# Sums of a seven-product FFN moved from VectorE into the accumulation of TensorE

## The chip, the cores and the metric

The kernel runs on one core of a Trainium2 chip. The metric is the device time of one execution in microseconds (us), lower is better; a comparison goes by the median of several runs. A separate execution is profiled, and all views of the profile and of its trace come from that one. PE is TensorE (PEld its weight loads), DVE is VectorE, ACT is ScalarE, POOL is GpSimd, SP is the engine that issues most DMAs.

## The reference

One decoder layer in float32 over x of 512 tokens x 1024: a half-step SwiGLU FFN, a token mixer of two kinds of recurrent heads, and a second half-step FFN, each with a norm before and after. The change is in the FFNs and in the step from the mixer to the second FFN.

```python
D_MODEL = 1024; SEQ = 512; D_FF = 2816
def rms_norm(x, g):
    xf = x.astype(jnp.float32)
    y = xf * lax.rsqrt(jnp.mean(xf * xf, axis=-1, keepdims=True) + EPS)
    return (y * g.astype(jnp.float32)).astype(x.dtype)

def swiglu_ffn(x, w_in, w_out):
    gate, up = jnp.split(x @ w_in, 2, axis=-1)
    return (jax.nn.silu(gate) * up) @ w_out

# per layer l
x = x + 0.5 * rms_norm(swiglu_ffn(rms_norm(x, norm_pre[l, 0]), ffn1_w_in[l], ffn1_w_out[l]), norm_post[l, 0])
mixed = token_mixer(rms_norm(x, norm_pre[l, 1]), w_mix_in[l], ...)
x = x + rms_norm(mixed, norm_post[l, 1])
x = x + 0.5 * rms_norm(swiglu_ffn(rms_norm(x, norm_pre[l, 2]), ffn2_w_in[l], ffn2_w_out[l]), norm_post[l, 2])
```

## The kernel before

**Products in two parts.** A float32 operand is split into a high part, rounded to the type that TensorE multiplies quickly (fp32r), and a low part, the rest. A product is three passes: high by high, high by low, low by high. For weights, ACT casts the high part (line 245) and DVE subtracts to get the low one (line 247); `split` does this, and four places (`WBUF`) in one tile hold split weights in turn. The raw weights come by DMA into rings of buffers.

**Seven products per pair.** The 2816 columns of gate and of up are taken in 11 pairs of 128-column chunks (t = 0 to 10). For one pair, the input is cut in two halves of tokens (256 each) and two halves of the model dimension (512 each), and the weights in a (upper rows, gate), b (upper rows, up), c (lower rows, gate), d (lower rows, up). The 2 x 2 block product is made of seven products p1 to p7 instead of eight, in Winograd's form, with sums of input blocks (s1 to s4, made once by `sums`) and sums of weights. The weight sums are made in place in the raw buffers (line 261): for t below `HEAD` = 3 by GpSimd, later by DVE. Pair 0 is made in the ordinary way (products c1 to c4 and e1 to e4), while the sums of the input are still in the making. One product is 24 matmuls of 128 x 128 by 256 (line 562) in `prod`; its result is one PSUM bank (128 x 512: two chunks of columns by 256 tokens). p2 adds to p1's bank and p4 to p5's.

**What follows a product** is in `after`. `h0` and `h1` are the two token halves of hf, the hidden activations of the pair. Before the change, in the names of the code (P1 for the result of p1):

- after p1, ACT copies P1 to h1; after p2, ACT puts Silu(P1 + P2) to h0;
- after p5, DVE writes u = P5 - P1 to SBUF;
- after p6, DVE writes q = P6 + u to SBUF, and h1 = q - P7;
- with p6 and p3 there, DVE adds q to p3's bank; with p2 there too, h0 = that bank times h0 is put on a list (`later`) that `lag` empties at the next product;
- after p4, DVE subtracts h1 from p5's bank, ACT takes its Silu in place, and h1 is multiplied by it, again by way of `later`.

**What sets the order.** The products come in the hand-written list `ORDER`; `HEADS` is its beginning. p4 of a pair stands in the next pair. In the steady pairs (t from 4 on) the order is p1, p4 of t - 1, p3, p5, p7, p6, p2. A scheduler puts each engine's instructions in an order before the run, with the program's order as the priority; each engine runs its own queue strictly in order, and semaphores make it wait for the others. PSUM has eight banks, handed out as they come free. `weights` works out from the list when each raw buffer's DMA may be issued.

**Between mixer and second FFN** stands `mix_out1`: the second 512 columns of the mixer's output product, for each of four tiles of 128 tokens. `last` runs the matmuls of a tile, then `post1` (the norm after, and x updated in two halves of 512 columns by line 457: first the half in SBUF, `y`, and then the half that still lies in a PSUM bank), then `pre` (the norm before the FFN: two squares summed on ACT, a power on GpSimd, a scaling on DVE). Then `ffn_head` begins the second FFN with c1, c3 and so on. For the last tile c1 runs meanwhile, and c3 follows the transposes of the third tile.

Of the kernel before, what the change touches and what calls it, by code (L numbers as in the profile page):

```python
# [38 lines left out]


HEAD = 3
HEADS = [("c1", 0), ("c3", 0), ("c2", 0), ("c4", 0), ("p1", 1), ("e1", 0), ("e3", 0)]
HEADS += [("e2", 0), ("p1", 2), ("p2", 1), ("e4", 0), ("p2", 2)]
ORDER = HEADS + [(p, 1) for p in ("p7", "p5", "p3", "p6")] + [("p5", 2), ("p7", 2), ("p3", 2), ("p4", 1), ("p6", 2)]
for _t in range(HEAD, PAIRS):
    if _t == HEAD:
        ORDER += [("p1", _t), ("p3", _t), ("p5", _t), ("p4", _t - 1)] + [(p, _t) for p in ("p7", "p6", "p2")]
    else:
        ORDER += [("p1", _t), ("p4", _t - 1)] + [(p, _t) for p in ("p3", "p5", "p7", "p6", "p2")]

# [35 lines left out]
class Layer:  # L88
# [257 lines left out]
    def sums(self, i, src):  # L346


        nc = self.nc
        v = slice((i % 2) * P, (i % 2 + 1) * P)  # L350
        f = [x[:, :, v] for x in self.xf]
        sub = lambda out, a, b: nc.vector.tensor_tensor(out, a, b, op=ALU.subtract)
        hi = lambda dst, src: nc.scalar.copy(dst[0][:, :, v], src)
        lo = lambda dst, src: sub(dst[1][:, :, v], src, dst[0][:, :, v].bitcast(F32))
        p1, p0 = self.turn(src, 1), self.turn(src, 0)
        a22 = self.hf[:, 10 + i, :].rearrange("p (c t) -> p c t", c=KH)
        s1, s2, s3, s4 = self.left["e1"], self.sq[2], self.sq[1], self.sq[0]
        a21, two = self.left["e1"], self.left["e2"]
        hi(a21, p0)
        hi(two, p1)  # L360
        nc.scalar.copy(a22, p1)
        lo(a21, p0)
        self.lowed = lo(two, p1)
        yield
        sub(p1, p0, a22)
        sub(p0, f[0], p0)
        hi(s3, p0)
        lo(s3, p0)
        yield
        sub(p0, f[0], p1)  # L370
        hi(s1, p1)
        lo(s1, p1)
        yield
        hi(s2, p0)
        sub(p1, f[1], p0)
        lo(s2, p0)
        yield
        hi(s4, p1)
        lo(s4, p1)
        yield  # L380
# [30 lines left out]
        self.pow = nc.gpsimd.tensor_tensor(r, b, self.nhalf[:, :1], op=ALU.pow)  # L411
        yield r

    def pre(self, i, g):

        r, xn = self.root(i)
        for h in range(2):
            self.scaled(i, g, r, xn, h)
        return xn

    def root(self, i):

        x = self.xs[:, i, :]
        *_, r = self.rms([x[:, :512], x[:, 512:]])
        if i % 2:
            xn = self.hf[:, 16:18, :].rearrange("p a t -> p (a t)")
        else:
            xn = self.sp.tile([P, D], F32, tag="xn", bufs=1, name=self.nm("xn"))
        return r, xn
# [16 lines left out]
    def post1(self, i, y, parts, rms, pieces, g, out=None):  # L446

        nc = self.nc
        for ps, v in pieces:
            parts.append(ps)  # L450
            next(rms)
            o = ps if out is None else out[:, v]
            nc.vector.tensor_tensor(o, ps, g[:, 512 + v.start : 512 + v.stop], op=ALU.mult)
        r = next(rms)
        for h, v in enumerate((y, pieces[0][0] if out is None else out)):
            x = self.xs[:, i, 512 * h : 512 * h + 512]
            added = nc.vector.scalar_tensor_tensor(x, v, r, x, op0=ALU.mult, op1=ALU.add)
        self.added = [self.square, added]
# [9 lines left out]
    def last(self, mm, ys, pieces, g, after, trans, head, out=lambda i: ()):  # L468


        for i in range(NT):
            for left in mm(i):
                if i == NT - 1 and left == 2:
                    trans(i - 2)
            self.post1(i, *ys[i], pieces(i), g, *out(i))
            after(i)
            if i == 2:
                trans(0)
        head(trans)

# [51 lines left out]
    def open_ffn(self, ctx):  # L534

        hp = self.hpool = ctx.enter_context(self.tc.tile_pool(name=self.nm("hp"), bufs=1))
        self.hf = hp.tile([P, NF, T], F32, name=self.nm("hf"))
        self.xf = [self.hf[:, j : j + 2, :].rearrange("p a (b t) -> p (a b) t", t=HALF) for j in (NF - 4, NF - 2)]
        sq = [hp.tile([P, 2 * D + PAD], F32R, tag="s", bufs=3, name=self.nm("sq")) for _ in range(3)]
        self.sq = [self.both(self.place(t, LATE)) for t in sq]  # L540
        xq = [self.both(x) for x in self.xh]
        self.stay = [self.place(t, NEXT) for t in sq]
        self.left = {"p1": xq[0], "p2": xq[1], "p4": xq[3], "p5": xq[2], "p6": self.sq[2], "p7": self.sq[1], "p3": self.sq[0]}
        self.left.update({"c1": xq[0], "c2": xq[1], "c3": xq[0], "c4": xq[1]})
        self.left.update({"e1": xq[2], "e2": xq[3], "e3": xq[2], "e4": xq[3]})
        self.gs, self.held, self.copies = [], {}, []
        self.hs, self.bank, self.later, self.u, self.q, self.had = deque(), {}, deque(), {}, {}, set()

    def prod(self, p, t, feed=True):

        w, left = self.held.pop("c" + p[1]) if p[0] == "e" else self.pull(feed), self.left[p]
        if p[0] == "c":
            self.held[p] = w
        into = {"p2": "p1", "p4": "p5", "c2": "c1", "c4": "c3", "e2": "e1", "e4": "e3"}.get(p, p)
        ps = self.bank[into, t] = self.bank.get((into, t)) or self.ps()
        first = into == p
        wb = self.both(w)
        for n, (b, d) in enumerate(((0, 0), (1, 0), (0, 1)) if p == "c1" else ((0, 0), (0, 1), (1, 0))):
            for a in range(2):
                c, v = slice(HALF * a, HALF * (a + 1)), slice(P * a, P * (a + 1))  # L560
                for k in range(KH):
                    self.nc.tensor.matmul(  # L562
                        ps[:, c], wb[b][:, k, v], left[d][:, k, :],
                        start=first and a + n + k == 0, stop=n == 2 and k == KH - 1, skip_group_check=True,
                    )
        if p[0] == "p" or p == "e2":
            self.drop(w)
        self.had.add((p, t))
# [8 lines left out]
    def after(self, p, t):  # L577
# [5 lines left out]
        if p in ("c2", "e2"):  # L583
            nc.scalar.activation(h0 if p == "c2" else h1, self.two_by(bank[p[0] + "1", t]), AF.Silu)
        elif p in ("c4", "e4"):
            h = h0 if p == "c4" else h1
            self.later.append(lambda: tt(h, self.two_by(bank[p[0] + "3", t]), h, ALU.mult))
        elif p == "p1":
            nc.scalar.copy(h1, self.two_by(bank["p1", t]))  # L589
        elif p == "p2":  # L590
            nc.scalar.activation(h0, self.two_by(bank["p1", t]), AF.Silu)
        elif p == "p4":
            ps = bank["p5", t]
            tt(self.two_by(ps), self.two_by(ps), h1, ALU.subtract)
            nc.scalar.activation(ps, ps, AF.Silu)
            self.later.append(lambda: tt(h1, self.two_by(ps), h1, ALU.mult))
        elif p == "p5":
            u = self.u[t] = self.st("u")
            tt(self.two_by(u), self.two_by(bank["p5", t]), h1, ALU.subtract)
        elif p == "p6":  # L600
            u = self.u.pop(t)
            q = self.q[t] = self.st("q")
            tt(q, bank["p6", t], u, ALU.add)
            tt(h1, self.two_by(q), self.two_by(bank["p7", t]), ALU.subtract)
        if p in ("p6", "p3") and {("p6", t), ("p3", t)} <= had:
            tt(bank["p3", t], self.q.pop(t), bank["p3", t], ALU.add)
        if p in ("p6", "p3", "p2") and {("p6", t), ("p3", t), ("p2", t)} <= had:
            self.later.append(lambda: tt(h0, self.two_by(bank["p3", t]), h0, ALU.mult))

    def lag(self):  # L610
        while self.later:
# [115 lines left out]
    def ffn_in(self):  # L727

        for p, t in ORDER[len(HEADS) :]:
            self.feed()  # L730
            self.lag()
            self.prod(p, t)
            self.after(p, t)
            if t == PAIRS - 1 and p in ("p7", "p6"):
                self.hs.append(self.h_tile(len(self.hs)))
        self.feed()
        self.lag()
# [277 lines left out]
    def ffn_items(self, name, w_in, w_out):  # L1015
# [5 lines left out]
        for t in range(1, PAIRS):  # L1021
            if t >= HEAD:
                v1, v3 = ("p1", t), ("p4", t - 1)
            elif t > 1:
                v1, v3 = ("p3", t - 1), ("p6", t - 1)
            else:
                v1, v3 = ("p1", 1), ("p1", 2)
            for at, o, i in ((("p5", t), "a", "d"), (("p6", t), "a", "c"), (v1, "a", "b"), (v3, "b", "d")):
# [9 lines left out]
        own = {("p1", t): [load(t, r) for r in "abdc"] for t in range(2, PAIRS)}  # L1038
        own["c1", 0] = [load(t, r, None if (t, r) == (0, "d") else name) for t in range(2) for r in "acbd"]

        stay = {"c1": 1, "c3": 2, "c4": 0}
        for p, t in ORDER:
            if p[0] == "e":
                continue
# [596 lines left out]
def layer(tc, aps):  # L1641
    with ExitStack() as ctx:
# [10 lines left out]
        def norm(i, row=None):  # L1653
            if i == 0 and row is not None:
                gp[0] = L.gain("gpre", pre[row : row + 1, :])
            xn[i] = L.pre(i, gp[0])

        def root(i):

# [76 lines left out]
```

## Time and profile before

| what | value |
|---|---|
| median of 3 runs | 943.95 us (943.27 to 944.35) |
| the profiled execution's own time | 944.65 us |
| its span, first to last instruction | 942.9 us |
| granted TensorE clock in it | 0.999 of full speed |
| PE, PEld busy | 934.1 us (99%), 900.4 us (95%) |
| DVE, ACT, POOL busy | 779.7 us (83%), 490.8 us (52%), 120.9 us (13%) |
| share of the chain that ended last | PE 62%, no other engine over 1% |
| HBM read, written | 92.85 MB, 2.10 MB |

How to read it: the slices divide the span in 40 equal parts, a digit being the busy tenths of an engine. A row of the timeline has the start (us from the span's start), the length, the engine, the line of the kernel, the operation, the tile written and those read, the shape and a count; in brackets the idle time of that engine ahead of it and who ended it. The row of a group of matmuls is longer than their pitch by the last one's way through the array, so ends are read from the next row's start. In the list of waits each row has the total, the number and the longest. The first FFN's input products run from about 12 to 226 us, the second's from about 608 to 820 us.

### The profile page before, as it was taken

How to read it: one execution, taken by the hardware profiler on the slowest of the kernel's cores; microseconds unless marked ns; L12 is line 12 of the kernel's file. 1: busy time of each engine (PE TensorE's matmuls, PEld its weight loads, DVE VectorE, ACT ScalarE, POOL GpSimd, SP SyncE). 2: the span in 40 equal slices, each digit the busy share in tenths (PEclk: the TensorE clock that was granted, in tenths of full speed). 3: DMA queues.
4: the chain of work that ended last, by engine and by line, in shares of the span. 5: the costliest groups of instructions: out<-in, count | busy, mean ns of one | idle time of the engine just before them, and what ended most of it. 6: DMA issues, size and time to landing. Idle time of an engine off the chain costs nothing.

```text
span 942.9 us, 18101 instructions
## 1 busy us (share of the span) xinstructions
PE 934.1 (99%) x7507; PEld 900.4 (95%) x7507; DVE 779.7 (83%) x1056; ACT 490.8 (52%) x695; POOL 120.9 (13%) x176
## 2 busy tenths in 40 slices
PE   9999999999999999999999999999999999999997
PEld 7999999999999999998887888899999999999997
DVE  6799989999888876698846665689998999998884
ACT  7645444456456467956632444664444444655541
POOL 2530000000001046200011310363100000000101
PEclk9999999999999999999999999999999999999999
DMA  9244333323352024321212124324333333223212
GB/s 318 86 135 134 110 116 113 112 90 90 99 171 90 24 85 126 107 67 47 88 46 67 46 90 140 103 71 132 115 113 106 119 113 112 68 90 128 75 46 90
DMA packets 81677, 96.13 MB, mean 102 GB/s; under 512 B 4117, under 2 KB 61497, under 8 KB 81594
## 3 DMA queue, kind: packets, MB, share of 16 engines
q1 hardware_dynamic: 81306, 94.44, 31.7%
q8 instruction: 59, 0.97, 0.4%
q10 hardware_dynamic: 288, 0.52, 0.2%
q14 instruction: 24, 0.20, 0.1%
HBM read 92.85 MB, written 2.10 MB: 101 GB/s over the span
## 4 chain that ended last, share of the span: by engine, by line
PE 62%; ACT 1%; DVE 1%; POOL 0%; issue 0%; POOLq 0%; DVEq 0%; ACTq 0%
PE ps L562 22%; PE ps L835 8%; PE ps L496 6%; PE ps L151 5%; PE ps L843 5%; PE ps L153 4%; PE ps L152 4%; PE ps L1226 2%; PE ps L506 1%; PE ps L319 1%; PE ps L1400 0%; PE ps L1311 0%; PE ps L1480 0%; PE ps L1507 0%; PE ps L1266 0%; ACT junk L406 0%
## 5 line engine op out<-in xcount | busy, mean ns | idle before, releaser
L245 ACT CAST w<-raw 128x1024 fp32r<-128x1024 f32 (+1 forms) x232 | 239.1, 1035 | 252.9 <-PE ps L562 102.5
L247 DVE TENSOR_TENSOR w<-raw,w 128x1024 fp32r<-128x1024 f32 (+1 forms) x232 | 286.1, 1240 | 35.8 <-ACT w L245 35.5
L562 PE MATMUL ps<-xq,w 128*128 128x256 f32 x2016 | 238.5, 277 | 0.0
L562 PEld LDWEIGHTS ps<-xq,w 128*128 128x128 f32 x2016 | 233.8, 188 | 0.2 <-ACT hf L589 0.2
L562 PE MATMUL ps<-sq,w 128*128 128x256 f32 x1440 | 170.5, 277 | 0.0
L562 PEld LDWEIGHTS ps<-sq,w 128*128 128x128 f32 x1440 | 166.8, 188 | 0.0
L835 PE MATMUL ps<-w,hs 128*128 128x256 f32 x1056 | 124.2, 276 | 0.0
L835 PEld LDWEIGHTS ps<-w,hs 128*128 128x128 f32 x1056 | 121.7, 188 | 0.0
L261 DVE TENSOR_TENSOR raw<-raw,raw 128x1024 f32<-128x1024 f32 x64 | 82.3, 1285 | 0.6
L151 PE MATMUL ps<-w,xq 128*128 128x512 f32 x192 | 78.9, 411 | 0.1
L152 PE MATMUL ps<-w,xq 128*128 128x512 f32 x192 | 74.8, 390 | 0.0
L153 PE MATMUL ps<-w,xq 128*128 128x512 f32 x192 | 74.8, 391 | 0.0
L407 POOL TENSOR_SCALAR col<-col 128x1 f32<-128x1 f32 x24 | 9.0, 374 | 493.7 <-ACT junk L406 493.6
L496 PE MATMUL ps<-xq,w 128*128 128x256 f32 x480 | 56.4, 278 | 0.0
L496 PEld LDWEIGHTS ps<-xq,w 128*128 128x128 f32 x480 | 55.2, 188 | 0.5 <-issue 0.5
L843 PE MATMUL ps<-w,hs 128*128 128x256 f32 x432 | 51.9, 276 | 0.0
L261 POOL TENSOR_TENSOR raw<-raw,raw 128x1024 f32<-128x1024 f32 x16 | 44.2, 2763 | 50.7 <-DVE w L247 41.4
L843 PEld LDWEIGHTS ps<-w,hs 128*128 128x128 f32 x432 | 50.3, 188 | 0.0
L754 ACT CAST hs<-hf 128x1024 fp32r<-128x1024 f32 x34 | 35.7, 1050 | 25.7 <-PE ps L843 14.1
L151 PEld LDWEIGHTS ps<-w,xq 128*128 128x128 f32 x192 | 36.1, 188 | 8.2 <-issue 0.9
L153 PEld LDWEIGHTS ps<-w,xq 128*128 128x128 f32 x192 | 36.0, 188 | 8.2 <-DVE xq L326 0.3
L755 DVE TENSOR_TENSOR hs<-hf,hs 128x1024 fp32r<-128x1024 f32 x34 | 41.6, 1224 | 1.5 <-ACT hs L754 1.5
(255 smaller groups left out, 1167.1 us busy)
## 6 DMA issues: line engine op xcount, KB each, us to landing
raw<-in_ffn_w_in_dram SPq DMA_DIRECT2D x88, 512.0 KB, 3.6
raw<-in_ffn_w_out_dram SPq DMA_DIRECT2D x44, 512.0 KB, 4.1
raw<-in_w_mix_in_dram SPq DMA_DIRECT2D x28, 512.0 KB, 3.6
raw<-in_w_mix_out_dram SPq DMA_DIRECT2D x8, 512.0 KB, 3.6
out_dram<-xs SPq DMA_DIRECT2D x8, 256.0 KB, 2.0
xs<-in_x_dram SPq DMA_DIRECT2D x6, 256.0 KB, 7.0
gpost<-in_norm_post_dram SPq DMA_DIRECT2D x3, 512.0 KB, 4.6
gpre<-in_norm_pre_dram SPq DMA_DIRECT2D x2, 512.0 KB, 4.0
```

Of the source, the lines that this page charges most:

```text
L151: mm(ps, sh, mh, start=start, stop=False, **kw)
L152: mm(ps, sh, ml, start=False, stop=False, **kw)
L153: mm(ps, sl, mh, start=False, stop=stop, **kw)
L245: nc.scalar.copy(hi, raw)
L247: self.low = nc.vector.tensor_tensor(lo, raw, hi.bitcast(F32), op=ALU.subtract)
L261: (nc.vector if late else nc.gpsimd).tensor_tensor(o, o, c, op=ALU.add)
L496: mm(ps[:, u0:u1], w[:, a, k, :], self.xop(k, b, u0, u1), start=k + n + m == 0, stop=k == ND - 1 and n == 2, skip_group_check=True,)
L562: self.nc.tensor.matmul(ps[:, c], wb[b][:, k, v], left[d][:, k, :], start=first and a + n + k == 0, stop=n == 2 and k == KH - 1, skip_grou ...
L754: self.nc.scalar.copy(hi, src)
L755: self.nc.vector.tensor_tensor(lo, src, hi.bitcast(F32), op=ALU.subtract)
L835: mm(out, a[kk][:, i * P : (i + 1) * P], w[:, b, kk, QUARTER * v : QUARTER * (v + 1)], start=begin and c == kk == n == 0, stop=kk == 1 and ...
L843: mm(ps[:, QUARTER * c : QUARTER * (c + 1)], A[a][:, c], B[b], start=begin and c == n == 0, stop=n == 2, skip_group_check=True,)
```

## The change

Five edits go together.

1. From the fifth pair on (t >= `FILLED` = 4), DVE writes P5 - P1 into a PSUM bank, and p6's matmuls start without clearing and add to it. ACT copies the bank to another one, on which p7 is added; p3 is added on the first one. ACT copies the bank of p7 to h1. The left operand of p7 has its sign turned, so that p7 is added where it was subtracted. For t below 4, DVE keeps the sums, in another arrangement with as many operations.
2. The order of products: after the heads p5(1), p5(2), p6(1), p6(2), p3(1), p7(1), p3(2), p4(1), p7(2), and from t = 3 on p1, p5, p4 of t - 1, p6, p2, p3, p7.
3. The tiles of the sums and of the weights kept for pair 0 are renamed, so that they come free in the order in which the output product takes them; the first two tiles for it are made after p3 and p7 of the last pair.
4. Two weight sums of pair 2 are tied to other products: a + b to p2(2) instead of p3(1), b + d to p6(1) as before.
5. In `mix_out1`, the update of x takes the half in the bank first, and the squares of the norm that follows take that half first as well (`turned`).

The diff, without hunks that only move comments:

```diff
 HEAD = 3
+FILLED = 4
 ...
-ORDER = HEADS + [(p, 1) for p in ("p7", "p5", "p3", "p6")] + [("p5", 2), ("p7", 2), ("p3", 2), ("p4", 1), ("p6", 2)]
+ORDER = HEADS + [("p5", 1), ("p5", 2), ("p6", 1), ("p6", 2), ("p3", 1), ("p7", 1), ("p3", 2), ("p4", 1), ("p7", 2)]
 for _t in range(HEAD, PAIRS):
-    if _t == HEAD:
-        ORDER += [("p1", _t), ("p3", _t), ("p5", _t), ("p4", _t - 1)] + [(p, _t) for p in ("p7", "p6", "p2")]
-    else:
-        ORDER += [("p1", _t), ("p4", _t - 1)] + [(p, _t) for p in ("p3", "p5", "p7", "p6", "p2")]
+    ORDER += [("p1", _t), ("p5", _t), ("p4", _t - 1)] + [(p, _t) for p in ("p6", "p2", "p3", "p7")]
 ...
-        s1, s2, s3, s4 = self.left["e1"], self.sq[2], self.sq[1], self.sq[0]
+        s1, s2, s3, s4 = self.left["e1"], self.sq[0], self.sq[2], self.sq[1]
 ...
-        sub(p0, f[0], p0)
+        sub(p0, p0, f[0])
 ...
-    def root(self, i):
+    def root(self, i, turned=False):
         x = self.xs[:, i, :]
-        *_, r = self.rms([x[:, :512], x[:, 512:]])
+        parts = [x[:, :512], x[:, 512:]]
+        *_, r = self.rms(parts[::-1] if turned else parts)
 ...
-        for h, v in enumerate((y, pieces[0][0] if out is None else out)):
+        for h, v in ((1, pieces[0][0]), (0, y)) if out is None else ((0, y), (1, out)):
 ...
-        self.left = {..., "p6": self.sq[2], "p7": self.sq[1], "p3": self.sq[0]}
+        self.left = {..., "p6": self.sq[0], "p7": self.sq[2], "p3": self.sq[1]}
 ...
         into = {"p2": "p1", "p4": "p5", "c2": "c1", "c4": "c3", "e2": "e1", "e4": "e3"}.get(p, p)
+        if p == "p3" and t >= FILLED:
+            into = "p6"
         ps = self.bank[into, t] = self.bank.get((into, t)) or self.ps()
-        first = into == p
+        first = into == p and (t < FILLED or p not in ("p6", "p7"))
 ...
-        elif p == "p5":
+        elif p == "p5" and t < FILLED:
             u = self.u[t] = self.st("u")
             tt(self.two_by(u), self.two_by(bank["p5", t]), h1, ALU.subtract)
+        elif p == "p5":
+            q = bank["p6", t] = self.ps()
+            tt(self.two_by(q), self.two_by(bank["p5", t]), h1, ALU.subtract)
+        elif p == "p6" and t < FILLED:
+            u = self.u[t]
+            tt(u, bank["p6", t], u, ALU.add)
         elif p == "p6":
-            u = self.u.pop(t)
-            q = self.q[t] = self.st("q")
-            tt(q, bank["p6", t], u, ALU.add)
-            tt(h1, self.two_by(q), self.two_by(bank["p7", t]), ALU.subtract)
-        if p in ("p6", "p3") and {("p6", t), ("p3", t)} <= had:
-            tt(bank["p3", t], self.q.pop(t), bank["p3", t], ALU.add)
-        if p in ("p6", "p3", "p2") and {("p6", t), ("p3", t), ("p2", t)} <= had:
-            self.later.append(lambda: tt(h0, self.two_by(bank["p3", t]), h0, ALU.mult))
+            c22 = bank["p7", t] = self.ps()
+            nc.scalar.copy(c22, bank["p6", t])
+        elif p == "p7" and t < FILLED:
+            tt(h1, self.two_by(bank["p7", t]), self.two_by(self.u[t]), ALU.add)
+        elif p == "p7":
+            nc.scalar.copy(h1, self.two_by(bank["p7", t]))
+        elif p == "p3" and t < FILLED:
+            c12 = bank["p6", t] = bank["p3", t]
+            tt(c12, self.u[t], c12, ALU.add)
+        if p in ("p3", "p2") and {("p3", t), ("p2", t)} <= had:
+            self.later.append(lambda: tt(h0, self.two_by(bank["p6", t]), h0, ALU.mult))
 ...
-            if t == PAIRS - 1 and p in ("p7", "p6"):
+            if t == PAIRS - 1 and p in ("p3", "p7"):
                 self.hs.append(self.h_tile(len(self.hs)))
 ...
             elif t > 1:
-                v1, v3 = ("p3", t - 1), ("p6", t - 1)
+                v1, v3 = ("p2", 2), ("p6", 1)
 ...
-        stay = {"c1": 1, "c3": 2, "c4": 0}
+        stay = {"c1": 2, "c3": 0, "c4": 1}
 ...
-            xn[i] = L.pre(i, gp[0])
+            xn[i] = L.pre(i, gp[0], row == 2)
```

More of the change, by code (lines that the diff above doesn't have):

```diff
@@ L412, in rms, with pre @@
         yield r
-    def pre(self, i, g):
-        r, xn = self.root(i)
+    def pre(self, i, g, turned=False):
+        r, xn = self.root(i, turned)
         for h in range(2):
@@ L542, in open_ffn @@
         self.stay = [self.place(t, NEXT) for t in sq]
-        self.left = {"p1": xq[0], "p2": xq[1], "p4": xq[3], "p5": xq[2], "p6": self.sq[2], "p7": self.sq[1], "p3": self.sq[0]}
+        self.left = {"p1": xq[0], "p2": xq[1], "p4": xq[3], "p5": xq[2], "p6": self.sq[0], "p7": self.sq[2], "p3": self.sq[1]}
         self.left.update({"c1": xq[0], "c2": xq[1], "c3": xq[0], "c4": xq[1]})
@@ L546, in open_ffn @@
         self.gs, self.held, self.copies = [], {}, []
-        self.hs, self.bank, self.later, self.u, self.q, self.had = deque(), {}, deque(), {}, {}, set()
+        self.hs, self.bank, self.later, self.u, self.had = deque(), {}, deque(), {}, set()
     def prod(self, p, t, feed=True):
```

## The prediction

> **What bounds the kernel now.** I read the page first: engines, slices, then the chain that ended last.
>
> ```profile
> span 942.9 us, 18101 instructions
> PE 934.1 (99%) x7507; PEld 900.4 (95%) x7507; DVE 779.7 (83%) x1056; ACT 490.8 (52%) x695; POOL 120.9 (13%) x176
> DVE  6799989999888876698846665689998999998884
> ```
>
> PE is busy for all but 8.8 us of the span, and DVE, which the change relieves, is near full in the slices of both FFNs. A busy DVE costs nothing unless PE waits for it, so the next view is the chain in order of time, where the second FFN is one long piece of PE.
>
> ```profile
> 617.59 0.87 PE ps L319 x8
> 618.47 201.99 PE ps L562 x1776
> ...
> 936.74 0.02 issue
> ```
>
> 1776 matmuls in 201.99 us are 0.1137 us each, so one product of 24 takes 2.73 us, with no hole between products. From 936.74 to the end 6.2 us are left, the tail behind the last matmul. So of the 8.8 us without a matmul most lie in the tail and in the start, which the change doesn't touch. PE's waits name what else there is.
>
> ```profile
> PE ps L147 <- POOL ident masks.py:199: 1.5, 1, 1.5
> PE ps L562 <- ACT junk L406: 0.4, 1, 0.4
> PE ps L562 <- ACT xq L339: 0.2, 1, 0.2
> ```
>
> The first, 1.5 us, is the making of the identity at the start. The second, 0.4 us, is at a place that the change edits (below). The whole stock from which it could win is thus about half a microsecond, and whatever new wait it puts on PE is paid in full. 0.2% of the median (943.95) is 1.9 us, about what a measurement of this kernel can tell from no change.
>
> **What the pairs lose on DVE.** Per pair from the fifth (t >= 4) line 581 made seven operations on DVE: the subtraction and the product of p4, u of p5, q and h1 of p6, the sum of p3, the product for h0. Now p6 and p3 accumulate in a bank that holds the sum already, and p7 (its left operand has its sign turned) in a copy, so u's operation goes into a bank, q, h1 and p3's sum go away, and ACT makes two copies more.
>
> ```profile
> 148.45 0.68 DVE L581 TENSOR_TENSOR hf<-q,ps 128x512 f32<-128x512 f32 x1
> 149.05 0.69 DVE L581 TENSOR_TENSOR ps<-q,ps 128x512 f32<-128x512 f32 x1
> 152.28 0.58 ACT L589 COPY hf<-ps 128x512 f32<-128x512 f32 x1
> 155.66 0.58 ACT L595 ACTIVATE ps<-ps 128x512 f32<-128x512 f32 x1 [0.54 <-DVE ps L581]
> ```
>
> One such operation holds DVE for 0.60 us (149.05 less 148.45). Three of them, seven pairs, two FFNs: 25 us off DVE. ACT gets 2 x 14 x 0.58 = 16 us more, where it has 452 us idle. PE's matmuls are as many as before; no row shows a matmul that is dearer when it adds onto a filled bank (each product's later passes add already), so I take nothing. On PE's path the sum of all this is nothing either: DVE's 25 us hide behind PE today.
>
> A copy from bank to bank is not in the trace of before. Its nearest rows are the copy from a bank to hf and the Silu from bank to bank, 0.58 both; I take 0.58. [...]
>
> **The new waits in the steady pairs.** The order becomes p1, p5, p4 of the pair before, p6, p2, p3, p7. Three waits are new.
>
> ```profile
> 141.07 5.60 PE L562 MATMUL ps<-sq,w 128*128 128x256 f32 x48
> 141.27 0.69 DVE L581 TENSOR_TENSOR u<-ps,hf 128x512 f32<-128x512 f32 x1 [0.75 <-PE ps L562]
> 146.51 8.38 PE L562 MATMUL ps<-xq,w 128*128 128x256 f32 x72
> ```
>
> p6 waits for DVE's filling. In this pair p5 ended where p7 began, at 141.07, and DVE was done with u at 141.96: 0.9 us. One product (p4) of 2.73 us lies between, so 1.8 us are to spare. p3 waits for ACT's copy out of the bank it will add to, with p2 between; p7 waits for the same copy, with p2 and p3 between. ACT's row at 152.28 is the copy after p1, which ended at about 152.0 (two products after 146.51): 0.3 + 0.58 = 0.9 us, again under 2.73. Behind DVE's and ACT's waiting instruction stand the next weight halves:
>
> ```profile
> 140.41 1.05 ACT L245 CAST w<-raw 128x1024 fp32r<-128x1024 f32 x1 [1.66 <-PE ps L562]
> 141.88 1.21 DVE L247 TENSOR_TENSOR w<-raw,w 128x1024 fp32r<-128x1024 f32 x1
> 143.12 1.22 DVE L261 TENSOR_TENSOR raw<-raw,raw 128x1024 f32<-128x1024 f32 x1
> ```
>
> Four weight places go round; the cast waits only for PE to leave one, and by the order of the products the half made at 141.88 to 143.09 is that of p1(7), which starts at 149.23: 6.1 us ahead. p5 now follows p1 directly, and its weights are p1's raw plus another, so its cast waits for p1's low half and the sum: 1.05 + 1.22 + 1.22 = 3.5 us after p1's cast instead of 2.73. It is some 0.8 us later, out of 6. Nothing reaches PE. Of the banks a pair takes four, where it took five, so no wait for a bank is added.
>
> **The fifth pair of the first FFN** is where DVE is behind.
>
> ```profile
> 92.10 0.69 DVE L581 TENSOR_TENSOR q<-ps,u 128x512 f32<-128x512 f32 x1
> 96.76 1.23 DVE L261 TENSOR_TENSOR raw<-raw,raw 128x1024 f32<-128x1024 f32 x1
> 97.44 2.88 PE L562 MATMUL ps<-sq,w 128*128 128x256 f32 x24
> 99.37 0.70 DVE L581 TENSOR_TENSOR ps<-ps,hf 128x512 f32<-128x512 f32 x1
> 100.16 2.88 PE L562 MATMUL ps<-xq,w 128*128 128x256 f32 x24
> 116.73 0.70 DVE L581 TENSOR_TENSOR ps<-ps,hf 128x512 f32<-128x512 f32 x1 [0.48 <-PE ps L562]
> ```
>
> p4(3) ended at 97.44 and its subtraction came at 99.37, 1.9 us late. In the new order that slot ends p5(4), and p6(4) begins at 100.16. With the same lag the filling ends at 100.07: just in time. Every sum of raws that the new order pulls ahead of it costs 1.22 us; with one (a += c for p6) PE would stand for 1.2 us. Below nothing it can't go. The lag row itself is the nearest, so I take 0.2 us and keep 0 to 1.3. A pair later the lag is gone (DVE idle before 116.73), and 1.8 us per pair are saved besides.
>
> **The join before the second FFN.**
>
> ```profile
> 607.56 3.00 PE L562 MATMUL ps<-xq,sq 128*128 128x256 f32 x24
> 610.24 0.74 DVE L457 SCALAR_TENSOR_TENSOR xs<-y,col,xs 128x512 f32<-128x512 f32 x1
> 610.39 1.03 PE L319 MATMUL ps<-ident,xn 128*128 128x128 f32 x8
> 610.90 0.75 DVE L457 SCALAR_TENSOR_TENSOR xs<-ps,col,xs 128x512 f32<-128x512 f32 x1
> 611.56 1.22 DVE L247 TENSOR_TENSOR sq<-raw,sq 128x1024 fp32r<-128x1024 f32 x1
> 611.79 3.08 PE L562 MATMUL ps<-xq,sq 128*128 128x256 f32 x24 [0.36 <-ACT junk L406]
> 614.99 1.42 DVE L433 SCALAR_TENSOR_TENSOR hf<-xs,col,gpre 128x512 f32<-128x512 f32 x2 [1.08 <-POOL col L411]
> 617.43 1.03 PE L319 MATMUL ps<-ident,hf 128*128 128x128 f32 x8
> ```
>
> The wait is put down to ACT, but the product c3 begins 0.14 us after DVE's second addition (610.90 + 0.75 = 611.65), the one that reads a bank: the bank is what c3 needs. With the bank's half first it is free at 610.99, before the eight transposes are through (611.26; eight take 0.87 us in the chain above). So c3 starts about 0.5 us sooner. What is late next: c3's low weights end at 612.78, wanted for its last eight matmuls at 613.1; the transposes at 617.43 would come at 616.9 and read what DVE ends at 616.41. Both hold, narrowly. The square that follows reads the half made first (turned), so its time stays. Gain: 0.5 us; from 0 (c3's bank is another) to 0.55. The tail keeps its old order.
>
> **The third pair and before.** The products after the heads are reordered, with as many operations for t < 4 as before. GpSimd's eight sums of raws per FFN come in another order, and those of p5(2) and p6(2) earlier.
>
> ```profile
> 53.01 5.84 POOL L261 TENSOR_TENSOR raw<-raw,raw 128x1024 f32<-128x1024 f32 x2 [8.93 <-DVE col L1074]
> 54.13 2.40 DVE L1078 TENSOR_TENSOR col<-col,col 128x4 f32<-128x4 f32 x1
> 59.59 2.35 DVE L247 TENSOR_TENSOR w<-raw,w 128x1024 fp32r<-128x1024 f32 x2
> 61.48 5.82 PE L562 MATMUL ps<-sq,w 128*128 128x256 f32 x48
> 67.28 3.31 POOL L261 TENSOR_TENSOR raw<-raw,raw 128x1024 f32<-128x1024 f32 x1 [8.42 <-DVE w L247]
> 68.37 4.57 DVE L261 TENSOR_TENSOR raw<-raw,raw 128x1024 f32<-128x1024 f32 x2
> 619.92 0.70 DVE L352 TENSOR_TENSOR ps<-ps,hf 128x512 f32<-128x512 f32 x1
> ```
>
> While GpSimd adds, a DVE operation on 4 columns takes 2.40 us. By the order of splits the first low half of 59.59 is for the product at 61.48: it ends at 60.8, with 0.7 us to spare, and 2.5 us counting that low halves are read in a product's last third. In the new order another of these sums (the one at 67.28) moves to before that product, and two more of line 581's operations (u's of p5(2), and p6(1)'s): 2.4 + 2 x 0.6 = 3.6 us against 2.5. But it leaves 68.37, where a DVE sum took about twice its 1.22. Bounds -0.2 (the third wait in PE's list, should it lie here) to +3.5 (the 3.6 with nothing to spare); I take nothing, as PE stood for nothing that the page lists under the same eight sums before. [...]
>
> **The sum**, against the profiled execution's 944.65 us (span 942.9 and 1.75 around it): -0.5 + 0.2 + 0 = -0.3. The median of the runs is 0.7 lower than that execution, so 943.95 - 0.3 = 943.6 us.
>
> **The rivals.**
> (a) GpSimd's sums and DVE's weights collide about 48 to 65 us, and PE waits there. For: the 0.7 us above, and DVE late by microseconds up to 100 us. Against: the second FFN, whose DVE is less late, and the low half's third. Price 1 to 3.5, less 0.3: 944.7 to 947.2; about 945.5. Chance 0.18, of which 0.12 beyond +1.9.
> (b) Slower in every pair: DVE's queue puts the filling behind a low half and a sum that are released at the same time. It decides from 1.8 us of delay. Price: 0.2 + 1.22 + 1.22 + 0.69 + 0.1 = 3.4 us against 2.73, 0.7 us in each of 14 pairs, 9.8 us: 953. For: the order of DVE's queue is fixed when the program is built, and low halves come every 2.73 us. Against: u, in the same place, began 0.2 us after p5 in the steady pairs. Chance 0.13.
> (c) c3's bank is another, or its weights hold it up: 944.1 us. Chance 0.03; against it, the 0.14 us.
> (d) Faster by over 1.9 us: PE would have to gain what no wait shows, some other hole between matmuls. 0.03, at 941.5.
>
> **How the numbers follow.** The forecast has 0.63; with (c) and the smaller part of (a), 0.72 lie within 0.2%. Slower is (b) and the larger part of (a), 0.25; faster 0.03. The range goes down to the full gain of join and heads with the median's own spread (942.8) and up to the middle of (a) with that spread (946.0); (b), the end of (a) and (d) are left out, about 0.2.
>
> **What would show it.** c3 begins near 611.3 if all before it stays; PE's waits show line 562 behind DVE's filling or ACT's copies for tenths at most; DVE's busy time falls by some 25 us with the span unmoved; ACT's rises by 16. Wrong would be: holes before p6 in each pair (b), holes near 50 to 65 us (a), or c3 still waiting for DVE (c).

## The result

| | median | runs | ratio to before |
|---|---|---|---|
| before | 943.95 us | 943.27 to 945.64, 7 runs | |
| after | 946.78 us | 945.98 to 947.72, 7 runs | 1.0028 (1.0018 to 1.0037) |
| after, run again beside before on another chip | 946.26 us (before 943.59) | 945.94 to 947.13, 6 runs | 1.0029 (1.0018 to 1.0041) |

The change makes the kernel slower, by 2.8 us (0.3%) in the first comparison and by 2.7 in the second. The forecast was 943.6, range 942.8 to 946.0. The profiled execution of after took 946.30 us, with a span of 944.6.

The page of after, engines and slices:

```profile
span 944.6 us, 18076 instructions
PE 933.8 (99%) x7507; PEld 899.4 (95%) x7507; DVE 756.6 (80%) x1014; ACT 504.3 (53%) x723; POOL 118.6 (13%) x176
```

DVE has 42 operations and 23 us less, ACT 28 and 13.5 us more, PE the same matmuls: the change does what it says. None of it was on PE's path. PE's waits show what is:

```profile
PE ps L145 <- POOL ident masks.py:199: 1.5, 1, 1.5
PE ps L565 <- DVE xq L339: 0.6, 1, 0.6
PE ps L565 <- ACT xq L337: 0.5, 2, 0.3
PE ps L565 <- DVE xs L457: 0.5, 1, 0.5
PE ps L565 <- DVE ps L584: 0.4, 1, 0.4
```

The columns are the total, the number and the longest. The last row is the fifth pair's p6, which waits for DVE's filling (line 584 is before's 581). The three above it lie at the join before the second FFN, but for 0.2 of the 0.5 us for ACT's `xq`: that wait ends at 12.0 us, at the head of the first FFN, where the kernel before has it too. (Lines 565, 457, 404, 432, 339, 337 and 245 of after are 562, 457, 406, 433, 341, 339 and 247 of before.)

**Where the 2.6 us lie.** Both kernels were profiled a second time (e9 and e10 below), 943.76 and 946.34 us. Four rows of the same place in each give the account. They are a product of pair 0 at the head of the first FFN, eight transposes after the first FFN, the long piece of the second FFN in the chain, and the last update of x. First before, then after:

```profile
41.74 2.88 PE L562 MATMUL ps<-xq,sq 128*128 128x256 f32 x24
335.65 1.03 PE L319 MATMUL ps<-ident,xn 128*128 128x128 f32 x8
617.61 201.98 PE ps L562 x1776
938.29 0.74 DVE L457 SCALAR_TENSOR_TENSOR xs<-hf,col,xs 128x512 f32<-128x512 f32 x1
span 942.1 us, 18101 instructions
```

```profile
41.69 2.88 PE L565 MATMUL ps<-xq,sq 128*128 128x256 f32 x24
336.21 1.03 PE L317 MATMUL ps<-ident,xn 128*128 128x128 f32 x8
619.63 201.98 PE ps L565 x1776
940.31 0.75 DVE L457 SCALAR_TENSOR_TENSOR xs<-hf,col,xs 128x512 f32<-128x512 f32 x1
span 944.6 us, 18076 instructions
```

| place | after less before |
|---|---|
| start (41.69 - 41.74) | -0.05 |
| first FFN (336.21 - 335.65, less the above) | +0.61 |
| mixer and join (619.63 - 617.61 = 2.02, less 0.56) | +1.46 |
| second FFN (201.98 both) and output (940.31 - 938.29 = 2.02) | 0.00 |
| tail behind the last update (944.6 - 942.1 = 2.5, less 2.02) | +0.5 |
| sum | +2.5 (own times: 946.34 - 943.76 = 2.58) |

The n-th matmul of one trace set against the n-th of the other narrows this down: all of the 0.61 arises between 97 and 115 us, 1.49 us between 604 and 613 us (the mixer ahead of it gives back 0.03), and the steady pairs of both FFNs differ by nothing.

**The join.** The third tile's update, its first square and its scaling, and c1 and c3, before (e9):

```profile
602.05 0.75 DVE L457 SCALAR_TENSOR_TENSOR xs<-y,col,xs 128x512 f32<-128x512 f32 x1 [0.19 <-POOL col L411]
602.71 0.75 DVE L457 SCALAR_TENSOR_TENSOR xs<-ps,col,xs 128x512 f32<-128x512 f32 x1
602.89 0.63 ACT L406 ACTIVATE junk<-xs 128x512 f32<-128x512 f32 x1 [1.47 <-DVE xs L457]
606.27 1.42 DVE L433 SCALAR_TENSOR_TENSOR xn<-xs,col,gpre 128x512 f32<-128x512 f32 x2 [1.62 <-POOL col L411]
606.72 3.00 PE L562 MATMUL ps<-xq,sq 128*128 128x256 f32 x24
610.96 1.77 PE L562 MATMUL ps<-xq,sq 128*128 128x256 f32 x13 [0.36 <-ACT junk L406]
```

and after (e10):

```profile
603.39 0.74 DVE L457 SCALAR_TENSOR_TENSOR xs<-y,col,xs 128x512 f32<-128x512 f32 x1
604.05 0.74 DVE L457 SCALAR_TENSOR_TENSOR xs<-ps,col,xs 128x512 f32<-128x512 f32 x1
604.90 0.63 ACT L404 ACTIVATE junk<-xs 128x512 f32<-128x512 f32 x1 [1.39 <-DVE xs L457]
607.71 2.10 PE L565 MATMUL ps<-xq,sq 128*128 128x256 f32 x16 [0.29 <-ACT xq L337]
608.28 1.42 DVE L432 SCALAR_TENSOR_TENSOR xn<-xs,col,gpre 128x512 f32<-128x512 f32 x2 [2.30 <-POOL col L409]
610.36 1.22 PE L565 MATMUL ps<-xq,sq 128*128 128x256 f32 x8 [0.55 <-DVE xq L339]
612.97 3.06 PE L565 MATMUL ps<-xq,sq 128*128 128x256 f32 x24 [0.51 <-DVE xs L457]
```

Two things are to be seen. DVE takes `xs<-y` before `xs<-ps`, as before: the code names the bank's half first, but the order in which DVE's instructions were put when the program was built does not follow it. ACT's squares do follow the code. The first now reads the half that DVE makes second: it starts 1.51 us after the first update (604.90 - 603.39), where it started after 0.84 (602.89 - 602.05). Square, power, scaling and the next tile's update hang on each other, so each tile adds 0.67 us of its own, and some 0.4 us of it reach the next tile's update: the third tile's update comes 1.34 us later than before (603.39 - 602.05) and its scaling 2.01 us later (608.28 - 606.27). Of both, 0.53 us were there ahead of the join; the 1.48 us that are left of the scaling are the loss.

### The profile page after: what moved, and what is told of

Same layout as the page of the kernel before. It is cut to its first block, busy times and chain, and to the rows that moved or that the text cites. A ratio compares the mean times of both kernels' runs of the same rounds, so it can differ in the third digit from the quotient of the medians.

```text
span 944.6 us, 18076 instructions
## 1 busy us (share of the span) xinstructions
PE 933.8 (99%) x7507; PEld 899.4 (95%) x7507; DVE 756.6 (80%) x1014; ACT 504.3 (53%) x723; POOL 118.6 (13%) x176
## 4 chain that ended last, share of the span: by engine, by line
PE 60%; DVE 2%; ACT 1%; POOL 1%; issue 1%; DVEq 0%; POOLq 0%; ACTq 0%
PE ps L565 22%; PE ps L847 7%; PE ps L497 6%; PE ps L855 5%; PE ps L149 4%; PE ps L151 4%; PE ps L150 4%; PE ps L1238 2%; PE ps L507 1%; ACT junk L404 1%; DVE xs L457 1%; PE ps L317 1%; PE ps L1412 0%; PE ps L1323 0%; PE ps L1519 0%
## 5 line engine op out<-in xcount | busy, mean ns | idle before, releaser
L259 DVE TENSOR_TENSOR raw<-raw,raw 128x1024 f32<-128x1024 f32 x64 | 78.3, 1224 | 1.8
L766 ACT CAST hs<-hf 128x1024 fp32r<-128x1024 f32 x34 | 35.7, 1051 | 20.9 <-PE ps L855 13.5
L259 POOL TENSOR_TENSOR raw<-raw,raw 128x1024 f32<-128x1024 f32 x16 | 42.1, 2637 | 28.3 <-DVE w L245 26.9
```

What stands on the lines that cost most here:

```text
L259: (nc.vector if late else nc.gpsimd).tensor_tensor(o, o, c, op=ALU.add)
L766: self.nc.scalar.copy(hi, src)
```

## The experiments

Each ran with a profile; medians are of 9 to 12 runs (e9 one, e10 six) beside 22 to 32 runs of the kernel before on the same chip (943.88, 943.72 and 943.59 us in the three sets). The expectations speak of the theories by letters: T and F say that the join, the fifth pair and the tail lose by the mechanisms above and below.

### e1: edit 5 undone

```diff
-        for h, v in ((1, pieces[0][0]), (0, y)) if out is None else ((0, y), (1, out)):
+        for h, v in enumerate((y, pieces[0][0] if out is None else out)):
-            xn[i] = L.pre(i, gp[0], row == 2)
+            xn[i] = L.pre(i, gp[0])
```

> The changed kernel with edit 5 undone (update of x and squares in the old order; DVE's instructions come in the same order as with the edit, so this takes away only the turned squares). Theory T: the join loses 1.47 us because the turned squares wait for DVE's second update (0.84 us after the start of that update instead of 0.17), tile after tile. Then c3 begins again some 0.5 us earlier than in the kernel before, and the median falls by 1.4 to 1.5 us from 946.8 to about 945.3. Rival R: the join is late because edits 1 to 4 left DVE and ACT in another order there; then the median stays at 946.8 and c3 stays at about 612.8.

Measured 944.77 us, ratio 1.0013 (1.0004 to 1.0022): 2.0 us under the changed kernel, somewhat more than expected. Between 583 and 640 us its matmuls lose nothing on those of the first profile of before (they gain 0.1 us). T holds for the lost time, and R does not; but T's half microsecond beyond that, c3 sooner than in the kernel before, did not come. As DVE's instructions stand in one order with and without the edit, it is the turned squares alone.

### e3: the kernel before with edit 5 alone

The same two lines the other way round, with `turned` carried through `pre` and `root`.

> The kernel before with edit 5 alone (DVE's order does not follow the code and keeps the SBUF half first; only the squares are turned). Theory T: slower by 1.4 to 1.5 us, 945.4, and the whole loss lies between 583 and 615 us of the trace. Rival R: 943.95, no change.

Measured 945.41 us, 1.0018 (1.0009 to 1.0027), as T said. Its rows:

```profile
603.52 0.74 DVE L458 SCALAR_TENSOR_TENSOR xs<-ps,col,xs 128x512 f32<-128x512 f32 x1
604.38 0.63 ACT L406 ACTIVATE junk<-xs 128x512 f32<-128x512 f32 x1 [1.38 <-DVE xs L458]
619.06 201.98 PE ps L563 x1776
```

The square waits for the second update (603.52 + 0.74 = 604.26) in a kernel that has none of the other edits, and the second FFN's long piece starts 1.45 us later than e9's (617.61). Edit 5 is thus the whole loss of the join, by addition as by removal.

### e2 and e7: the bank's half really first

```diff
+        firsts = []
         for h, v in ((1, pieces[0][0]), (0, y)) if out is None else ((0, y), (1, out)):
             x = self.xs[:, i, 512 * h : 512 * h + 512]
-            added = nc.vector.scalar_tensor_tensor(...)
+            with self.behind(*firsts):
+                added = nc.vector.scalar_tensor_tensor(...)
+            firsts = [added] if out is None else []
```

> The changed kernel in which the update of the SBUF half is tied behind that of the bank's half, so that DVE really takes the bank's half first; the squares stay turned. Theory T (squares wait for whichever update comes second in DVE's queue): the square starts 0.2 us after the first update again, the join gives back its 1.47 us and wins up to 0.5 more because c3's bank is free one update (0.65 us) earlier: 944.8 to 945.3. Rival R (the order of the two updates doesn't matter, the join is late for what edits 1 to 4 did): 946.8.

Measured 945.24 us, 1.0017 (1.0008 to 1.0026): the lost time is back, but it is no better than e1. The trace shows why:

```profile
610.97 0.74 DVE L459 SCALAR_TENSOR_TENSOR xs<-y,col,xs 128x512 f32<-128x512 f32 x1
611.20 3.04 PE L568 MATMUL ps<-xq,sq 128*128 128x256 f32 x24
613.92 1.42 DVE L432 SCALAR_TENSOR_TENSOR hf<-xs,col,gpre 128x512 f32<-128x512 f32 x2 [1.08 <-POOL col L409]
615.26 1.22 DVE L245 TENSOR_TENSOR w<-raw,w 128x1024 fp32r<-128x1024 f32 x1
616.53 1.20 PE L568 MATMUL ps<-xq,w 128*128 128x256 f32 x8 [0.48 <-DVE w L245]
```

c3 now starts while DVE is still at the second update, so it was the update that frees the bank which held c3, and not the later one. But the fourth tile's scaling has come ahead of c2's low weights in DVE's order, and c2's last eight matmuls wait 0.48 us for them. e7 ties that scaling behind the low weights (it moves the two calls of `scaled`, and what follows from them, into `ffn_head`, under `behind(self.low)`):

> As e2 (bank's half really first, squares turned), and the scaling of the fourth tile tied behind the second of the low halves that the head of the second FFN makes, so that c2's low weights are not late as they were in e2 (0.48 us of waiting and 0.2 before). Theory: c3 begins about 0.55 us sooner than in the kernel before, and nothing later takes that back, so the join gives 1.45 + 0.55 = 2.0 us against the changed kernel: 944.8 us, 0.4 below e2 (945.2). Rival: what comes next is late instead (the transposes of the fourth tile, which read the scaling); then c4 starts as in the kernel before and the median is 945.3.

Measured 944.98 us, 1.0010 (1.0001 to 1.0018), between the two expectations. Its list of waits has nothing of the join, and between 583 and 640 us its matmuls gain 0.36 us on those of the first profile of before. But 0.15 of that lies behind 617 us, and e4 and e5, whose join has the fault, gain it there too; ahead of 613 us it is 0.2 us. That is what doing the edit as meant is worth, where 0.5 was forecast.

### e4: the fifth pair's sums left on DVE

```diff
-FILLED = 4
+FILLED = 5
```

> The changed kernel with the sums of the fifth pair left on DVE (bound 5 instead of 4, in both FFNs). Theory T: the 0.65 us that PE loses at 98 to 105 us while p6(4) waits for DVE's filling go away, and nothing comes in their place: 946.15. Rival R2: DVE is late there anyway, and the sixth pair's filling or the fifth pair's later operations stop PE by as much: 946.8.

Measured 945.88 us, 1.0023 (1.0013 to 1.0033), 0.9 under the changed kernel. No wait for line 584 is in PE's list, and between 97 and 115 us its matmuls lose nothing on e9's: T. The profiles show what the loss depends on. Rows of the first profile of after:

```profile
97.70 1.22 DVE L245 TENSOR_TENSOR w<-raw,w 128x1024 fp32r<-128x1024 f32 x1
98.83 0.69 DVE L584 TENSOR_TENSOR ps<-ps,hf 128x512 f32<-128x512 f32 x1
99.58 2.66 PE L565 MATMUL ps<-sq,w 128*128 128x256 f32 x21 [0.36 <-DVE ps L584]
```

The filling comes behind a low half and ends at 99.52; p6's turn on PE was at 99.05. In the other profiles in which PE waited (e2, e5, e7, e10, e12) the filling ends between 99.27 and 99.62, while p6's turn lies between 98.71 and 99.32: the sooner PE comes, the longer it waits. In e1 PE came to the fifth pair 1.4 us later than here, after the filling's end at 100.27, and did not wait at all; in e12 it came 0.1 us sooner than here and waited 0.5. The filling itself took its usual 0.69 us.

### e5: the tail

From the last update's end to the span's end takes 942.06 - 939.03 = 3.0 us before (e9) and 944.61 - 941.05 = 3.6 after (e10). The DMA view of 938 to 945 us of e10 has one row that e9's lacks, an instruction packet, and its two output DMAs land later (us in the last column); e9's row for them is the third:

```profile
q14 instruction: 1, 0.01, 0.4%
out_dram<-xs SPq DMA_DIRECT2D x2, 256.0 KB, 2.3
out_dram<-xs SPq DMA_DIRECT2D x2, 256.0 KB, 2.0
```

The packet has 8192 bytes, starts at 942.09 and lasts 0.40 us, beside the packets of the last output. e5 gives SP more to issue ahead of it:

```diff
-            for h in range(2):
-                v = slice(512 * h, 512 * h + 512)
+            n = 8 if i < 2 else 2
+            for h in range(n):
+                v = slice(D // n * h, D // n * (h + 1))
```

> The changed kernel whose first two output tiles are stored in eight pieces each instead of two: 12 more DMA issues on SP, long before the end. The last output DMA took 2.0 us from issue to landing in the kernels with the old edits 1 to 4 left out and 2.5 to 2.6 in those with them, and beside it lies one 8 KB instruction packet of 0.45 us in the latter alone. Theory F: the program of SP has 22 instructions less and so SP's last fetch of instructions falls on the last output DMA; with 24 or so instructions more it falls some 10 us earlier, the tail is 0.6 us shorter, and the median falls from 946.8 to 946.2. Rival: the longer landing has another reason (where the tile of x lies, the state of the queues); the tail stays at 7.1 us and the median at 946.8.

```profile
940.17 0.74 DVE L457 SCALAR_TENSOR_TENSOR xs<-hf,col,xs 128x512 f32<-128x512 f32 x1
span 944.0 us, 18090 instructions
```

With 14 instructions more the packet starts at 931.5 us, and the tail is 944.0 - 940.9 = 3.1 us, as before the change. Theory F holds in the trace: it is SP's fetch. The other profiles bear it out. SP has 368 instructions in the trace before, 360 with edits 1 to 4 and the split stores, and 346 with edits 1 to 4 and the stores as they were, and the last such packet starts at 907 to 912, 930 to 932 and 941 to 942 us. The tail is 3.6 to 3.7 us in the six profiles in which it falls on the last output, and 3.0 to 3.1 in the other eight. The median does not show it: 947.25 us, 1.0028 (1.0017 to 1.0038), where 946.2 was expected. The nine runs lie in two groups, four at 945.7 to 945.9 and five at 947.2 to 948.5; the changed kernel's fastest were 945.98 and 945.94. The times alone would not decide it.

The trace has two queues that carry instructions alone: q8, with 59 packets of 16384 bytes in both kernels, and q14, the one in question, with 24 of 8192 bytes before and 23 after (within the span).

### e6, e8 and e12: taken together

e6 is e1, e4 and e5 in one kernel, e12 is e1 and e5, and e8 is e7, e4 and e5.

> The changed kernel with edit 5 undone, the sums of the fifth pair left on DVE, and the first two output tiles stored in eight pieces. If the loss of 2.8 us is the sum of three places (join 1.45, fifth pair 0.65, tail 0.6), the median is that of the kernel before, 943.9 (943.7 to 944.2). Rival: some 0.5 us or more lies elsewhere in the steady pairs or in the heads, and it stays at 944.4 or above.

> The changed kernel with edit 5 undone and the first two output tiles stored in eight pieces, the fifth pair's sums in TensorE's banks: what is left is the order of products and the filled banks. Theory: all that it loses is the fifth pair's wait, 0.6 to 1.2 us with the slower matmuls behind it: fastest runs at 943.7 to 944.2, median near 944.6, against 944.04 of e6. Rival: the fifth pair's wait is only seen where PE comes early, and the median is that of e6 and of the kernel before.

> e7 with the sums of the fifth pair on DVE and the first two output tiles stored in eight pieces: all three losses away and the join's gain kept. Theory: 943.9 - 0.55 = 943.35 us, 0.06% below the kernel before, less than a run can tell. Rival, join's gain taken back: 943.9.

e6: 944.04 us, 0.9999 (0.9990 to 1.0007): with the three places undone the rest of the change costs nothing that can be measured. e12: 944.20 us, 1.0005 (0.9996 to 1.0014); PE's list has the fifth pair's wait again:

```profile
PE ps L565 <- DVE ps L584: 0.5, 1, 0.5
```

Its fastest run (943.85) lies 0.75 above e6's (943.10), as expected, but its median is 0.4 under the expected 944.6, and its interval would not tell it from no change. What decides is the trace: its matmuls lose 0.75 us on e9's between 97 and 100 us, where e6's lose nothing. e8: 945.21 us, 1.0006 (0.9997 to 1.0015), inconclusive. Five of its twelve runs lie at 943.1 to 943.8 and six at 945.2 to 945.7; the profiled one is of the second group, and 1.7 us of it lie in the mixer (last section).

### e9, e10 and e11

> The kernel before once more, for another profile. In its first profile PE stood for 0.4 us at 43.7 us (line 562 behind ACT's copy to hf) and then took 117.8 ns per matmul instead of 113.3 until 75 us, 1.4 us in all; none of the kernels made since shows this, e3 with the same FFNs included. Theory P (an accident of that execution, which was 0.7 above the median): no stall there, 113.3 ns from 45 us on, and a time near 943.3. Rival: it belongs to the old order of the heads; then it is there again and the time is near 944.6.

e9, one run: 943.76 us, without the wait and without the slow stretch. Theory P for the slow stretch. The wait is no accident of that one execution: e12, which has the new order of the heads, waits 0.3 us at the same place. Behind it e12 has no slow stretch.

> The changed kernel once more, beside the kernel before on the same chip. Theory: the loss is join 1.45, fifth pair 0.6 to 1.2 (p6 of the fifth pair starts at about 99.5 us, when the filling is done, however early PE came there) and tail 0.6: the fastest runs lie at 943.1 + 2.7 to 2.9 = 945.9, the median at 946.5 to 947, with a second group some 1.5 us above the first as in the other kernels. Rival: the loss is not stable, and the median lies within 1.5 us of the kernel before.

e10: in the table at the top, 0.2 under the expected median; the loss is stable.

> The kernel before with edit 5 done as it was meant and mended: bank's half first in DVE's queue, squares turned, the scaling of the fourth tile behind the second low half. Nothing of the other edits. Theory: c3 starts 0.5 us sooner and 0.35 us of it is kept (as between 583 and 640 us of e7): 943.5 where the kernel before has 943.85. Rival, nothing is kept: 943.85. Both lie within what a run can tell; the trace decides between them.

e11: 943.38 us against 943.59, 0.9997 (0.9989 to 1.0006): no difference that can be told. In its trace the second low half (612.56) comes before the scaling (614.58). The eight transposes, the fourth tile's first update and c3:

```profile
609.89 1.03 PE L319 MATMUL ps<-ident,xn 128*128 128x128 f32 x8
610.10 0.75 DVE L460 SCALAR_TENSOR_TENSOR xs<-ps,col,xs 128x512 f32<-128x512 f32 x1
611.00 3.03 PE L566 MATMUL ps<-xq,sq 128*128 128x256 f32 x24
617.63 201.83 PE ps L566 x1776
```

c3 starts 0.15 us after the end of the update that frees its bank (610.10 + 0.75), as it did in the kernel before. The update itself comes late: in e2, e7 and e11 DVE has taken one of the two `xq` low parts ahead of the third tile's update (in e11 at 601.95), which puts that tile's update 0.3 us later, with all that follows; and the fourth tile's update of the bank's half begins only 0.1 us after the end of the operation that writes what it reads, which the other half needn't wait for, so that it comes 0.5 us later. From 583 to 640 us e11 gains 0.37 us on the first profile of before, as e7 does, of which 0.15 are the shorter last row, 201.83 (no slow matmuls in it). It is the best of the versions tried, but not shown to beat the kernel before.

## Why the prediction was wrong

- **What bounds the kernel**: right. DVE's 23 us (25 were forecast; on ACT 13.5, where 16 were forecast) brought nothing: the second FFN's 1776 matmuls take 201.98 us in both. What the new waits cost was paid in full: the 2.02 us by which PE is behind at 619.63 are still there at the last update (940.31 against 938.29).
- **Steady pairs**: right. 1776 matmuls take 201.98 us in both; rival (b) is absent. A copy from bank to bank takes 0.58 us, as taken:

```profile
102.54 0.58 ACT L611 COPY ps<-ps 128x512 f32<-128x512 f32 x1
```

- **The join**: here the forecast failed, taken at -0.5 and measured at +1.46. Two steps failed. "With the bank's half first it is free at 610.99" took the order of the code for that of DVE's queue, though rival (b) spoke of a queue whose order is fixed when the program is built. "The square that follows reads the half made first (turned), so its time stays" rested on the first: with DVE's order unchanged, turning made each square wait for the half made second. Only the fourth tile was looked at, no row of a square was, and no rival had a loss at the join. The mechanism that was named, the bank that holds c3, is real (e2, e7, e11). But it was worth 0.2 us, not 0.5: c3's hold-up behind the transposes falls by 0.3 us and c1 loses 0.16, since the chain ahead of them runs 0.3 us later in DVE's new order (e11). That c3 would start at the transposes' end did not come true either; it still waits for the bank.
- **The fifth pair**: right in kind, mis-sized. It was taken at 0.2 with bounds of 0 and 1.3; measured 0.61. In e10 0.2 of it are the wait with the first matmul, and 0.4 slower matmuls behind it; in the first profile of after the wait alone took 0.5 from start to start (0.4 in the list) and the next matmul 0.1 more than its pitch. "Just in time" was read from a profile in which PE was itself late, behind the slow stretch described below. The same two rows in e9:

```profile
99.16 0.69 DVE L581 TENSOR_TENSOR ps<-ps,hf 128x512 f32<-128x512 f32 x1
99.36 2.88 PE L562 MATMUL ps<-xq,w 128*128 128x256 f32 x24
```

  Here DVE is done at 99.85, 0.5 us after the slot's end, so the same reading of e9 would have given a wait of 0.5. That e10 waited 0.2 is no sign that the forecast of 0.2 was well founded.
- **The heads**: right at 0. e10 and e9 differ by 0.05 at 42 us and by as little at 97. Rival (a) is absent.
- **The tail**: "which the change doesn't touch" failed by 0.5. Its instructions are the same, but SP has 22 fewer in all, and a fetch moved onto the last output.
- **The own time**: the first profiled execution of before was 0.9 longer than that of e9, for the slow stretch below. Its distance to the median was subtracted as a whole, which came out right by luck: what made that execution long was not known.

The sum that the runs support is 0 + 0.61 + 1.46 + 0 + 0.5 = 2.6, against -0.3.

## What to carry to other kernels

Where a scheduler sets an engine's order, an order written in the code is a wish (in e10 the half named second began at 603.39 us, the one named first at 604.05): look in the trace at which of two instructions came first, and don't reverse a reader's order on another engine unless the writer's is tied. Where PE is busy for 99% of the span, look for what relief of another engine can win in PE's waits for it (here 23 us off DVE won nothing). A filling that must be there before a product is a new deadline (PE waited 0.36 us for it in the first profile of after); start it where that engine is not yet behind. How far an engine is behind PE is read in more than one profile. A gain under 0.2% is judged in the trace, place by place, against a second profile of the kernel before, because executions of one kernel differ by as much (the kernel before by 943.27 to 945.64 us, 0.25%).

## What was not expected of the hardware

**Two paces of matmul.** Most of the 128x256 matmuls come every 113.3 ns or every 117.8 ns, at a granted clock of 0.998 to 0.999 of full speed, in stretches of tens of matmuls up to some hundreds. In the first profile of before PE lost 0.3 us to a wait at 43.7 us (with the slower start behind it), and the stretch from 44 to 74 us ran at 117.8. The same product there and in e9, before the same small matmul of line 1069:

```profile
44.05 3.09 PE L562 MATMUL ps<-xq,w 128*128 128x256 f32 x24
44.46 2.88 PE L562 MATMUL ps<-xq,w 128*128 128x256 f32 x24
```

The wait and the pace together are the 1.4 us by which that execution fell behind e9 between 42 and 75 us. Of all the other profiles only e12 loses anything there, 0.3 us by the wait alone. In e8 most of 355 to 404 us ran so: 240 of line 500's matmuls lie in 359 to 387 us, where e6 has 250 (line 497).

```profile
L500 PE MATMUL ps<-xq,w 128*128 128x256 f32 x240 | 28.4, 281 | 0.0
L497 PE MATMUL ps<-xq,w 128*128 128x256 f32 x250 | 28.5, 276 | 0.0
```

Behind the fifth pair's wait the slow pace lasted 11 to 13 us in e5, e7 and e10 and was not there in e2, e12 and the first profile of after; e5 and e12 waited equally long, 0.6 us. So a short wait may cost its length again behind it (e10: 0.2 us of waiting, 0.4 behind it), but does not always (e12: 0.6 us and no slow matmuls), and its length does not decide it. What starts and ends the slow pace stays open. It may be what sets the two groups of runs in e5 and e8 apart, as it lengthened two of the profiles by 1.1 and 1.7 us; this was not tried, and the granted clock is 0.998 to 0.999 in both groups.

**Instruction fetches.** One of 8 KB beside the last output DMAs made their landing 0.3 us longer (median of two, e10 against e9) and the tail 0.5 to 0.7 us (e5), so a change far from the end can move the end (here 22 fewer instructions on SP).
